# Changing the edges of an MLP stage in an encoder kernel: split rooms, PSUM banks, put-off sums and a free order

## The chip, the cores and the metric

The kernel runs on one core of a Trainium2 chip. The metric is the device time of one execution in microseconds. The kernel before took 2067.26 us, the median of three runs (2062.96 to 2069.44).

## The reference

It is a trunk of two layers over 256 tokens of width 2048. Each layer is a pre-norm token mixer (12 heads, in layer 0 neighbourhood attention and in layer 1 grouped-query attention) beside 4 cross-attention heads into 256 memory tokens, one output projection, and then the part that this change is about, a squared-ReLU MLP of width 8192:

```python
for i in range(DEPTH):
    n = rms_norm(h, attn_norm[i])
    ...
    h = h + jnp.concatenate([mix, cross], axis=-1) @ w_o[i]
    n = rms_norm(h, mlp_norm[i])
    h = h + jnp.square(jax.nn.relu(n @ w_up[i])) @ w_down[i]
return rms_norm(h, final_norm)
```

All inputs and weights are float32.

## The kernel before

**Number format.** Every matrix product is done as three matmuls in fp32r. Each operand is split into a high part (a copy rounded to fp32r, on ACT, line 370) and a low part (the difference, on DVE, line 371), and hi x hi, hi x lo and lo x hi are summed in PSUM. A `split` is that pair. The weights come from DRAM as float32 in chunks of 1 MB, each in two halves of 128x1024, and every weight half is split before the PE can use it.

**The up projection.** `up_grains` makes 128 rows of the MLP's inner layer: `load` fetches a 1 MB chunk `raw_U` through the SP queue into one of two tiles, `prep(hf)` splits a half of it into `uh` and `ul`, and `run(hf)` does 24 matmuls of 128x256 with the normalized activations hT into the sum `ps_u`. `half_of_side` gives the rooms for the halves: `uh` and `ul` have two rooms each. `squared` then takes the sum (Relu on line 811, square on line 812, both on ACT) and from each second chunk makes sums and differences of the blocks (line 821, DVE) and splits them into `a`. `PARTS` is 8: an MLP is eight parts of eight such chunks (`PK`).

**The down projection.** For seven of the eight parts it is done by Strassen's scheme: four blocks of weights `b` and their combinations give seven products `p1` to `p7`, each with a PSUM bank of its own. `down_grains` does one step: `load` fetches `b` (two tiles), `pre` makes three sums in `t` (lines 845, 847, 848, on DVE) and adds one block to another with an accumulating DMA on the POOL queue (line 846), `prep_first` splits `b` into `bh` and `bl`, `prep_second` splits `t` into `th` and `tl` (one room each), and two runs do the products of FIRST (p3, p1, p2, p5: twelve matmuls of 128x512) and of SECOND (p7, p6, p4: nine). When a half of the columns ends, `taken` empties the banks: three products go straight into the residual h (line 905), four into the shared sums `z` (line 916). At the last time for a half, `folded` combines the z tiles into h with eight operations on DVE (lines 927 to 934). The eighth part goes through `plain_grains`, ordinary products of 128x512 into the sums `ps_m`.

**The order of the work.** `plan` is a list of grains. `run_all` walks it and calls each grain's load, pre and prep a fixed number of grains ahead (`SOON`: 8, 5 and 4), then its `run` and `after`. `later(n, fn)` puts a function off by n grains. First come the 16 halves of part 0 (the "first part" in this text), then 56 fused steps, each of a `down_grains` pair for one part and an `up_grains` pair for the next, in this order:

```python
            plan.extend((down[0], up[0], up[1], down[1]))
```

The framework then plans the order of the instructions on each engine by its own estimates of their times. `pin` (`keep_in_program_order`) holds instructions in the order in which they were written, `past(fn, split)` holds what `fn` issues behind a given split on its engine. In the fused steps the first matmul of each product and each k tile is pinned; in the first part nothing is. Each engine runs its own list strictly in the order so planned.

**PSUM.** Eight banks. Outside the MLP's fused steps, the pool `ps_acc` (four banks, opened first) holds sums such as `ps_u` of part 0 and `ps_m`, and `ps_att` (four banks) holds what attention and the transposes need. For the fused steps both are closed and `ps_sums` takes their place, with one bank for each of p4, p3, p1, p2, p5, p7, p6 in this order and one for `up`. A tile in a new pool waits for the last use of the tile whose bank it takes. A pool of SBUF works in the same way: `mlp` takes the space of `ring` and `cat` when they are closed.

Of the kernel before, what the change touches and what calls it, by code (L numbers as in the profile page):

```python
# [17 lines left out]
P = 128  # L18
D = 2048
SEQ = 256  # L20
# [21 lines left out]
MOVING_AT = 160  # L42

LAST_AT = 224

STILL_AT = 64

# [58 lines left out]
def encoder_kernel(ctx: ExitStack, tc: tile.TileContext, t: dict, out: bass.AP):  # L106
# [20 lines left out]
    class at:  # L127
        pass

    def open_sums():  # L130
        at.acc = opened("ps_acc", space=bass.MemoryType.PSUM, bufs=4)
        at.att = opened("ps_att", space=bass.MemoryType.PSUM, bufs=4)

    def open_ring():
        at.ring = opened("ring")
# [232 lines left out]
    def split(dst_hi, dst_lo, src):  # L368

        first = nc.scalar.activation(dst_hi, src, AF.Copy)  # L370
        return first, nc.vector.tensor_tensor(dst_lo, src, dst_hi.bitcast(F32), op=ALU.subtract)  # L371
# [393 lines left out]
    def half_of_side(raw, hf, place=0):  # L765
        s = slice(place // 4, place // 4 + HALF)
        tiles = tuple(at.side.tile([P, HALF + 64], F32R, tag=n, bufs=2, name=n)[:, s] for n in ("uh", "ul"))
        box.setdefault("splits", []).append(split(*tiles, raw[:, hf * HALF : (hf + 1) * HALF]))
        return tiles
# [3 lines left out]
        nc.sync.dma_start(raw, src)  # L773
        return raw

    def up_grains(layer, part, m):
        own = {}

        def load():
            own["raw"] = loaded(t[f"w_up{layer}"][part * PK + m], "U")  # L780

        def prep(hf):
            own[hf] = half_of_side(own["raw"], hf)

        def run(hf):
            if hf == 0:
                if part == 0:
                    own["ps"] = at.acc.tile([P, 512], F32, tag="acc", name="ps_u")[:, :SEQ]
                else:
                    own["ps"] = at.sums.tile([P, 512], F32, tag="up", name="ps_u")[:, :SEQ]  # L790
            products(own["ps"], box["hT"], hf * (KT // 2), KT // 2, *own.pop(hf), keep_order=part > 0)

        def after():
            if part == 0 and m == 0:
                closed("cat", "ring")
                at.mlp = opened("mlp")
                box["z"] = [at.mlp.tile([P, 4, 512], F32, tag=f"z{q}", name=f"z{q}") for q in range(2)]
                box["z_set"] = set()
# [26 lines left out]
        if part == PARTS - 1 and m == PK - 1 and layer == 1:  # L825
            later(2, load_gf)

    def down_grains(layer, part, n, begins, ends):

        q, j = part % 2 ^ n // STEPS, n % STEPS  # L830
        own = {}

        def load():
            own["b"] = at.side.tile([P, 4, 512], F32, tag="b", bufs=2, name="b")
            nc.sync.dma_start(own["b"].rearrange("p a b -> p (a b)"),
                              t[f"w_pair{layer}"][(part * 2 + q) * STEPS + j])

        def behind(fn):

            return (lambda: past(fn, box["splits"][-4])) if part == 0 and n < 2 else fn  # L840

        def pre():

            b, s = own["b"], at.side.tile([P, 3, 512], F32, tag="T", bufs=2, name="t")
            nc.vector.tensor_tensor(s[:, 0, :], b[:, 3, :], b[:, 0, :], op=ALU.add)  # L845
            nc.gpsimd.dma_start(b[:, 3, :], b[:, 1, :], accum_op=ALU.add)  # L846
            nc.vector.tensor_tensor(s[:, 1, :], s[:, 0, :], b[:, 1, :], op=ALU.add)
            nc.vector.tensor_tensor(s[:, 2, :], s[:, 1, :], b[:, 2, :], op=ALU.add)
            own["t"] = s

        def prep_first():
            own["first"] = tuple(at.mlp.tile([P, CH], F32R, tag=x, name=x) for x in ("bh", "bl"))
            split(*own["first"], own["b"].rearrange("p a b -> p (a b)"))

        def prep_second():
            own["second"] = tuple(at.mlp.tile([P, 3 * 512], F32R, tag=x, name=x) for x in ("th", "tl"))
            split(*own["second"], own["t"].rearrange("p a b -> p (a b)"))

        def run(which, products):
            if part == n == 0 and which == "first":  # L860
                closed("ps_att", "ps_acc")
                at.sums = opened("ps_sums", space=bass.MemoryType.PSUM)
                box["ps"] = {}
                box["unused"] = set()
            hi, lo = own.pop(which)
            a = box["a", part, j]
            for name, ai, bi in products:
                if begins:
                    sum_of(name)
                ps, s = box["ps"][name], slice(bi * 512, (bi + 1) * 512)  # L870
                pin(nc.tensor.matmul(ps, a[:, 0, ai, :], hi[:, s], start=begins, stop=False))  # L871
                nc.tensor.matmul(ps, a[:, 0, ai, :], lo[:, s], start=False, stop=False)  # L872
                nc.tensor.matmul(ps, a[:, 1, ai, :], hi[:, s], start=False, stop=ends)  # L873

        def after(products):
            if ends:
                for name, _, _ in products:
                    taken(q, name)

        def after_second():  # L880
            after(SECOND)
            if ends:
                box["z_set"].add(q)
            if ends and (part, n) in FOLDS:
                folded(q)

        return [Grain(lambda: run("first", FIRST), lambda: after(FIRST), load, behind(pre), behind(prep_first), SOON),
                Grain(lambda: run("second", SECOND), after_second, None, None, behind(prep_second), SOON)]

    def sum_of(name):  # L890

        if not box["ps"]:
            for x in ("p4", "p3", "p1", "p2", "p5", "p7", "p6"):
                box["ps"][x] = at.sums.tile([P, 512], F32, tag=x, name=x)
                box["unused"].add(x)
        if name in box["unused"]:
            box["unused"].remove(name)
        else:
            box["ps"][name] = at.sums.tile([P, 512], F32, tag=name, name=name)

    def columns_of(i, q, b):
        return h[:, i, q * 1024 + b * 512 : q * 1024 + (b + 1) * 512]

    def add_scaled(hs, src, factor):
        nc.vector.scalar_tensor_tensor(hs, src, factor, hs, op0=ALU.mult, op1=ALU.add)
# [14 lines left out]
    DIRECT = {"p2": (1, 0), "p3": (1, 1), "p4": (0, 0)}  # L920
    SHARED = ("p1", "p5", "p6", "p7")

    def folded(q):

        z1, z5, z6, z7 = (box["z"][q][:, n, :] for n in range(4))
        inv, ninv = box["inv"], box["ninv"]
        add_scaled(columns_of(1, q, 0), z1, inv[:, 1:2])
        nc.vector.tensor_tensor(z6, z6, z1, op=ALU.subtract)
        nc.vector.tensor_tensor(z7, z6, z7, op=ALU.subtract)
        nc.vector.tensor_tensor(z6, z6, z5, op=ALU.add)  # L930
        add_scaled(columns_of(1, q, 1), z6, inv[:, 1:2])
        add_scaled(columns_of(0, q, 0), z7, inv[:, 0:1])
        nc.vector.tensor_tensor(z7, z7, z5, op=ALU.add)
        add_scaled(columns_of(0, q, 1), z7, ninv[:, 0:1])

    def plain_grains(layer, nb):

# [17 lines left out]
        def begin():  # L955
            if nb == 0:
                closed("ps_sums")
                open_sums()
            w.ps = [at.acc.tile([P, 512], F32, tag="acc", name="ps_m") for _ in range(NT)]

        def run(n):
# [24 lines left out]
    SOON = (8, 5, 4)  # L986
    STEPS_OF = [(p, n) for p in range(PARTS - 1) for n in range(2 * STEPS)]
    HALF_OF = [p % 2 ^ n // STEPS for p, n in STEPS_OF]
    FOLDS = {STEPS_OF[max(i for i, x in enumerate(HALF_OF) if x == q)] for q in range(2)}

    def add_mlp(layer):
        for m in range(PK):
            plan.extend(up_grains(layer, 0, m))
        for x, (p, n) in enumerate(STEPS_OF):
            begins = x == 0 or HALF_OF[x - 1] != HALF_OF[x]
            ends = x == len(STEPS_OF) - 1 or HALF_OF[x + 1] != HALF_OF[x]
            up, down = up_grains(layer, p + 1, n), down_grains(layer, p, n, begins, ends)
            plan.extend((down[0], up[0], up[1], down[1]))
        for nb in range(4):
            plan.extend(plain_grains(layer, nb))  # L1000

# [301 lines left out]
```

## Time and profile before

| | |
|---|---|
| median of 3 runs | 2067.26 us (2062.96 to 2069.44) |
| profiled execution | 2065.99 us, of it 2064.2 us from the first to the last instruction |
| mean granted TensorE clock | 0.995 |
| PE (matmul) busy | 2034.1 us, 99% |
| DVE busy | 1663.7 us, 81% |
| ACT busy | 1243.8 us, 60% |
| moved by DMA | 433.83 MB, 210 GB/s in the mean |

The page slices the span and gives busy time for each engine. A matmul's busy time includes its way through the array, so that consecutive matmuls overlap and an almost unbroken busy time does not say that the PE is at its peak; the spacing of the starts does. In layer 0 the first part runs from about 438 us to 492, the fused steps to 1067 and the plain part after that; in layer 1 the same stages are at about 1374 to 1428, to 2008, and on to the end.

### The profile page before, as it was taken

Reading aid. Unit: us, or ns where it says so; the run is one execution under the profiler, and the core shown is the slowest. Engines: PE = TensorE matmul, PEld = TensorE weight load, DVE = VectorE, ACT = ScalarE, POOL = GpSimd, SP = SyncE. Lnnn points to the kernel's source line nnn. Section 1 sums busy time; section 2 is a strip of 40 time slices with the busy share of each in tenths; the row PEclk is TensorE's granted clock in tenths of the full one; section 3 lists DMA queues with packets and bytes.
Section 4 is the critical chain, followed back from the end, with each engine's and each line's share of the span. In section 5 each row is a group of like instructions: output and inputs, shape, how many; then the busy total and the mean of one; then the engine's idle time right before and its main releaser. Section 6 shows DMA issues by size and latency. Waiting matters only on the chain.

```text
span 2064.2 us, 32575 instructions
## 1 busy us (share of the span) xinstructions
PE 2034.1 (99%) x13116; PEld 1844.1 (89%) x13116; DVE 1663.7 (81%) x2030; ACT 1243.8 (60%) x1616; POOL 119.3 (6%) x144
## 2 busy tenths in 40 slices
PE   9999999999999999999999999999999999999988
PEld 8999999888999999999988888888999999999976
DVE  6767666557999999999996668657999999999985
ACT  6654444455666666666655557555666666666654
POOL 0000000000000000001000001000000000000000
PEclk9999999999999999999999999999999999999999
DMA  7855555726777777777765544626777777777762
GB/s 281 306 182 175 184 182 168 291 76 210 230 228 237 222 245 229 222 239 228 230 196 203 178 177 143 228 95 204 228 232 230 231 230 233 225 235 229 229 212 103
DMA packets 77303, 433.83 MB, mean 210 GB/s; under 512 B 8672, under 2 KB 10336, under 8 KB 29664
## 3 DMA queue, kind: packets, MB, share of 16 engines
q1 hardware_dynamic: 59760, 399.25, 55.5%
q0 software_dynamic: 16816, 31.46, 8.7%
q8 instruction: 102, 1.67, 0.3%
q10 hardware_dynamic: 576, 1.05, 0.1%
q14 instruction: 49, 0.40, 0.1%
HBM read 398.17 MB, written 4.19 MB: 195 GB/s over the span
## 4 chain that ended last, share of the span: by engine, by line
PE 73%; DVE 1%; DMA 1%; issue 1%; ACT 1%; POOLq 0%; POOL 0%; ACTq 0%; DVEq 0%
PE ps_u L286 31%; PE p L871 9%; PE p L872 9%; PE p L873 8%; PE ps_m L265 5%; PE ps_m L268 5%; PE ps_m L269 5%; DMA b<-b 1%; DVE ul L371 1%; PE pt_n L388 0%; PE pt_a L447 0%; DMA raw_U<-in_w_up 0%; ACT bh L370 0%; ACT uh L370 0%; PE pt_h L1087 0%
## 5 line engine op out<-in xcount | busy, mean ns | idle before, releaser
L286 PE MATMUL ps_u<-hT,uh 128*128 128x256 f32 x4096 | 713.3, 278 | 0.8 <-ACT uh L370 0.6
L286 PEld LDWEIGHTS ps_u<-hT,uh 128*128 128x128 f32 x4096 | 629.2, 189 | 10.7 <-ACT uh L370 1.6
L286 PE MATMUL ps_u<-hT,ul 128*128 128x256 f32 x2048 | 569.5, 278 | 8.1 <-DVE ul L371 8.1
L370 ACT ACTIVATE uh<-raw_U 128x1024 fp32r<-128x1024 f32 x278 | 294.6, 1061 | 309.6 <-PE ps_u L286 276.3
L286 PEld LDWEIGHTS ps_u<-hT,ul 128*128 128x128 f32 x2048 | 386.8, 189 | 9.8 <-DVE ul L371 9.6
L371 DVE TENSOR_TENSOR ul<-raw_U,uh 128x1024 fp32r<-128x1024 f32 x278 | 338.9, 1221 | 60.9 <-ACT uh L370 60.7
L371 DVE TENSOR_TENSOR lo<-raw,hi 128x1024 fp32r<-128x1024 f32 (+1 forms) x215 | 255.6, 1194 | 144.2 <-ACT hi L370 143.0
L370 ACT ACTIVATE hi<-raw 128x1024 fp32r<-128x1024 f32 (+1 forms) x215 | 222.1, 1039 | 201.0 <-PE ps_m L269 111.8
L370 ACT ACTIVATE bh<-b 128x2048 fp32r<-128x2048 f32 x112 | 215.2, 1922 | 122.3 <-PE p L873 87.7
L371 DVE TENSOR_TENSOR bl<-b,bh 128x2048 fp32r<-128x2048 f32 x112 | 256.3, 2289 | 22.2 <-ACT bh L370 22.1
L371 DVE TENSOR_TENSOR tl<-t,th 128x1536 fp32r<-128x1536 f32 x112 | 196.7, 1756 | 42.1 <-ACT th L370 41.1
L370 ACT ACTIVATE th<-t 128x1536 fp32r<-128x1536 f32 x112 | 166.7, 1488 | 38.7 <-PE p L873 38.7
L871 PE MATMUL p<-bh,a_s 128*128 128x512 f32 x448 | 175.2, 391 | 3.5 <-ACT c L811 1.9
L872 PE MATMUL p<-bl,a_s 128*128 128x512 f32 x448 | 175.0, 391 | 1.8 <-DVE bl L371 1.8
L873 PE MATMUL p<-bh,a_s 128*128 128x512 f32 x448 | 175.3, 391 | 0.0
L846 POOL DMA_DIRECT2D b<-b x112 | 97.0, 866 | 1157.0 <-DVE t L845 902.7
L286 PE MATMUL ps_s<-nT,hi 128*128 128x256 f32 x896 | 158.1, 279 | 0.0
L286 PEld LDWEIGHTS ps_s<-nT,hi 128*128 128x128 f32 x896 | 136.3, 188 | 0.2
L871 PE MATMUL p<-th,a_s 128*128 128x512 f32 x336 | 131.4, 391 | 0.0
L872 PE MATMUL p<-tl,a_s 128*128 128x512 f32 x336 | 131.2, 390 | 0.0
L873 PE MATMUL p<-th,a_s 128*128 128x512 f32 x336 | 130.7, 389 | 0.0
L286 PE MATMUL ps_s<-nT,lo 128*128 128x256 f32 x448 | 124.9, 279 | 0.0
(233 smaller groups left out, 3361.9 us busy)
## 6 DMA issues: line engine op xcount, KB each, us to landing
raw_U<-in_w_up SPq DMA_DIRECT2D x128, 1024.0 KB, 5.1
b<-in_w_pair SPq DMA_DIRECT2D x112, 1024.0 KB, 5.1
raw<-in_w_o SPq DMA_DIRECT2D x32, 1024.0 KB, 5.0
b<-b POOLq DMA_DIRECT2D x112, 256.0 KB, 3.4
raw<-in_w_b SPq DMA_DIRECT2D x21, 1024.0 KB, 5.1
raw<-in_w_av SPq DMA_DIRECT2D x12, 1024.0 KB, 5.0
raw<-in_w_aq SPq DMA_DIRECT2D x12, 1024.0 KB, 4.9
raw<-in_w_ak SPq DMA_DIRECT2D x12, 1024.0 KB, 4.9
```

The source lines that it names most:

```text
L265: first = nc.tensor.matmul(w.ps[i], ah, hi[:, s], start=st, stop=False)
L268: nc.tensor.matmul(w.ps[i], ah, lo[:, s], start=False, stop=False)
L269: nc.tensor.matmul(w.ps[i], al, hi[:, s], start=False, stop=sp)
L286: ins = nc.tensor.matmul(ps, x[:, s], acts[:, k, part], start=k == n == 0, stop=k == KT - 1 and n == 2)
L370: first = nc.scalar.activation(dst_hi, src, AF.Copy)
L371: return first, nc.vector.tensor_tensor(dst_lo, src, dst_hi.bitcast(F32), op=ALU.subtract)
L846: nc.gpsimd.dma_start(b[:, 3, :], b[:, 1, :], accum_op=ALU.add)
L871: pin(nc.tensor.matmul(ps, a[:, 0, ai, :], hi[:, s], start=begins, stop=False))
L872: nc.tensor.matmul(ps, a[:, 0, ai, :], lo[:, s], start=False, stop=False)
L873: nc.tensor.matmul(ps, a[:, 1, ai, :], hi[:, s], start=False, stop=ends)
```

## The change

- Part 0's halves, counted 0 to 15, use a third room where the count modulo 3 is 2. For half 2 it is a `b` tile (two tiles are shared with the down weights); for halves 5, 8, 11 and 14 it is the tiles `th` and `tl`, at an offset of 96 bytes (`U_AT`). The pool `mlp`, which holds `th` and `tl`, is opened before part 0's first matmuls instead of after its first chunk.
- In `ps_sums` the banks go by group: FIRST's four, and `up` with SECOND's three. In layer 0 the second group takes the four lower banks, in layer 1 the upper ones. When the pools of four are opened again after layer 0's MLP, `ps_att` is opened ahead of `ps_acc`, so the two change sides.
- `folded` issues its eight operations one at a time, one or two grains apart, each held behind a recent split.
- In the last four fused steps of each layer (from `LAST_HALF` on) no matmul is pinned, and the order of the grains is up, down, up, down.

```diff
+U_AT = 96
...
-    def open_sums():
-        at.acc = opened("ps_acc", space=bass.MemoryType.PSUM, bufs=4)
-        at.att = opened("ps_att", space=bass.MemoryType.PSUM, bufs=4)
+    def open_sums(layer=1):
+        for x in ("acc", "att")[:: 1 if layer else -1]:
+            setattr(at, x, opened(f"ps_{x}", space=bass.MemoryType.PSUM, bufs=4))
...
-    def up_grains(layer, part, m):
+    def up_grains(layer, part, m, fixed=False):
...
         def prep(hf):
-            own[hf] = half_of_side(own["raw"], hf)
+            if part == 0 and (2 * m + hf) % 3 == 2:
+                if m == 1:
+                    room = at.side.tile([P, 2, HALF], F32R, tag="b", bufs=2, name="u_b")
+                    own[hf] = room[:, 0], room[:, 1]
+                else:
+                    s = slice(U_AT // 4, U_AT // 4 + HALF)
+                    own[hf] = tuple(at.mlp.tile([P, 3 * 512], F32R, tag=x, name=f"u_{x}")[:, s] for x in ("th", "tl"))
+                box["splits"].append(split(*own[hf], own["raw"][:, hf * HALF : (hf + 1) * HALF]))
+            else:
+                own[hf] = half_of_side(own["raw"], hf)
         def run(hf):
+            if part == m == hf == 0:
+                closed("cat", "ring")
+                at.mlp = opened("mlp")
+                ...
             if hf == 0:
                 if part == 0:
                     own["ps"] = at.acc.tile([P, 512], F32, tag="acc", name="ps_u")[:, :SEQ]
                 else:
-                    own["ps"] = at.sums.tile([P, 512], F32, tag="up", name="ps_u")[:, :SEQ]
-            products(own["ps"], box["hT"], hf * (KT // 2), KT // 2, *own.pop(hf), keep_order=part > 0)
+                    own["ps"] = sum_of("up")[:, :SEQ]
+            products(own["ps"], box["hT"], hf * (KT // 2), KT // 2, *own.pop(hf), keep_order=fixed)
...
-    def down_grains(layer, part, n, begins, ends):
+    def down_grains(layer, part, n, begins, ends, fixed):
...
             if part == n == 0 and which == "first":
-                closed("ps_att", "ps_acc")
-                at.sums = opened("ps_sums", space=bass.MemoryType.PSUM)
-                box["ps"] = {}
-                box["unused"] = set()
+                open_strassen(layer)
...
-                pin(nc.tensor.matmul(ps, a[:, 0, ai, :], hi[:, s], start=begins, stop=False))
+                ins = nc.tensor.matmul(ps, a[:, 0, ai, :], hi[:, s], start=begins, stop=False)
+                if fixed:
+                    pin(ins)
...
             if ends and (part, n) in FOLDS:
-                folded(q)
+                folded(q, 1 if (part, n) == STEPS_OF[-1] else 2)
...
+    def open_strassen(layer):
+        closed(*[x for x in reversed(list(pools)) if x in ("ps_acc", "ps_att")])
+        at.sums = opened("ps_sums", space=bass.MemoryType.PSUM)
+        first = [x[0] for x in FIRST]
+        second = ["up"] + [x[0] for x in SECOND]
+        box["ps"], box["unused"] = {}, set()
+        for x in first + second if layer else second + first:
+            box["ps"][x] = at.sums.tile([P, 512], F32, tag=x, name="ps_u" if x == "up" else x)
+            box["unused"].add(x)
...
-    def folded(q):
+    def folded(q, gap):
...
+        for n, fn in enumerate((out(1, 0, z1, inv), add(z6, z6, z1, ALU.subtract), add(z7, z6, z7, ALU.subtract),
+                                add(z6, z6, z5), out(1, 1, z6, inv), out(0, 0, z7, inv), add(z7, z7, z5),
+                                out(0, 1, z7, ninv))):
+            later(1 + gap * n, lambda fn=fn: past(fn, box["splits"][-2]))
...
                 closed("ps_sums")
-                open_sums()
+                open_sums(layer)
...
+    LAST_HALF = max(i for i, x in enumerate(HALF_OF) if x != HALF_OF[-1]) + 1
...
-            up, down = up_grains(layer, p + 1, n), down_grains(layer, p, n, begins, ends)
-            plan.extend((down[0], up[0], up[1], down[1]))
+            fixed = x < LAST_HALF
+            up, down = up_grains(layer, p + 1, n, fixed), down_grains(layer, p, n, begins, ends, fixed)
+            plan.extend((down[0], up[0], up[1], down[1]) if fixed else (up[0], down[0], up[1], down[1]))
```

More of the change, by code (lines that the diff above doesn't have):

```diff
@@ L782, in prep @@
         def prep(hf):
-            own[hf] = half_of_side(own["raw"], hf)
-        def run(hf):
+            if part == 0 and (2 * m + hf) % 3 == 2:
[8 more added lines that the diff above has]
+                own[hf] = half_of_side(own["raw"], hf)
+        def run(hf):
+            if part == m == hf == 0:
+                closed("cat", "ring")
+                at.mlp = opened("mlp")
+                box["z"] = [at.mlp.tile([P, 4, 512], F32, tag=f"z{q}", name=f"z{q}") for q in range(2)]
+                box["z_set"] = set()
             if hf == 0:
@@ L789, in run @@
                 else:
-                    own["ps"] = at.sums.tile([P, 512], F32, tag="up", name="ps_u")[:, :SEQ]
-            products(own["ps"], box["hT"], hf * (KT // 2), KT // 2, *own.pop(hf), keep_order=part > 0)
+                    own["ps"] = sum_of("up")[:, :SEQ]
+            products(own["ps"], box["hT"], hf * (KT // 2), KT // 2, *own.pop(hf), keep_order=fixed)
         def after():
[L794 to L798, printed above, removed]
             squared(layer, part, m, own["ps"])
@@ L884, in after_second @@
             if ends and (part, n) in FOLDS:
-                folded(q)
+                folded(q, 1 if (part, n) == STEPS_OF[-1] else 2)
         return [Grain(lambda: run("first", FIRST), lambda: after(FIRST), load, behind(pre), behind(prep_first), SOON),
                 Grain(lambda: run("second", SECOND), after_second, None, None, behind(prep_second), SOON)]
+    def open_strassen(layer):
[7 more added lines that the diff above has]
+            box["unused"].add(x)
     def sum_of(name):
[L892 to L895, printed above, removed]
         if name in box["unused"]:
@@ L898, in sum_of @@
         else:
-            box["ps"][name] = at.sums.tile([P, 512], F32, tag=name, name=name)
+            box["ps"][name] = at.sums.tile([P, 512], F32, tag=name, name="ps_u" if name == "up" else name)
+        return box["ps"][name]
     def columns_of(i, q, b):
@@ L921, in encoder_kernel, with add, out @@
     SHARED = ("p1", "p5", "p6", "p7")
-    def folded(q):
+    def folded(q, gap):
         z1, z5, z6, z7 = (box["z"][q][:, n, :] for n in range(4))
         inv, ninv = box["inv"], box["ninv"]
[L927 to L934, printed above, removed]
+        def add(d, x, y, op=ALU.add):
+            return lambda: nc.vector.tensor_tensor(d, x, y, op=op)
+        def out(i, b, z, factor):
+            return lambda: add_scaled(columns_of(i, q, b), z, factor[:, i : i + 1])
+        for n, fn in enumerate((out(1, 0, z1, inv), add(z6, z6, z1, ALU.subtract), add(z7, z6, z7, ALU.subtract),
+                                add(z6, z6, z5), out(1, 1, z6, inv), out(0, 0, z7, inv), add(z7, z7, z5),
+                                out(0, 1, z7, ninv))):
+            later(1 + gap * n, lambda fn=fn: past(fn, box["splits"][-2]))
     def plain_grains(layer, nb):
```

## The prediction

> **What bounds the kernel now.** I read the page first, then the busy time of the engines by stage, then the PE's order of time wherever a stage had PE time missing, then the ACT, DVE and SP orders around those places.
>
> ```profile
> span 2064.2 us, 32575 instructions
> PE 2034.1 (99%) x13116; PEld 1844.1 (89%) x13116; DVE 1663.7 (81%) x2030; ACT 1243.8 (60%) x1616; POOL 119.3 (6%) x144
> ```
>
> The PE is the bound, so only its holes can be won. By stage (columns: length, then busy us and instructions of PE, PEld, DVE, ACT, POOL; granted clock, DMA share, GB/s):
>
> ```profile
> 495.37:1066.80 571.43, 571.43 (x3852) 525.40 (x3851) 528.28 (x561) 370.84 (x371) 46.14 (x53) 1.00 0.74 229
> 451.31:476.78 25.47, 25.47 (x219) 25.47 (x217) 17.04 (x24) 14.67 (x21) 1.05 (x1) 1.00 0.60 203
> 447.44:491.72 44.28, 39.39 (x312) 38.57 (x313) 32.77 (x46) 24.63 (x34) 2.80 (x3) 0.96 0.64 203
> 1383.34:1428.08 44.74, 39.55 (x312) 38.31 (x312) 2.90 (x8) 0.96 0.61 200
> ```
>
> (The last row counts the up matmuls alone.) Layer 0's fused up and down steps (571 us) have no hole, and the DVE is 92% busy there: 571.43 - 528.28 = 43 us of slack over about 56 steps, 0.8 us a step. The holes lie at the edges. In the first part 451.31 to 476.78 is nine undisturbed halves, 2.83 us each. The next two rows hold thirteen halves each, 36.8 us at that pace, but take 44.28 and 44.74: **7.5 us lost in layer 0, 7.9 in layer 1**. Where, on the PE (start, duration, then in brackets the idle time and what ended it):
>
> ```profile
> 482.48 0.38 PE L286 MATMUL ps_u<-hT,ul 128*128 128x256 f32 x1 [2.02 <-DVE ul L371]
> 493.18 0.50 PE L871 MATMUL p<-bh,a_s 128*128 128x512 f32 x1 [0.60 <-ACT c L811]
> 1428.08 0.50 PE L871 MATMUL p<-bh,a_s 128*128 128x512 f32 x1 [1.30 <-ACT c L811]
> 1066.57 0.39 PE L872 MATMUL p<-tl,a_s 128*128 128x512 f32 x1
> 1066.80 0.39 PE L873 MATMUL p<-th,a_s 128*128 128x512 f32 x1
> 1069.10 0.47 PE L265 MATMUL ps_m<-uh,a_p 128*128 128x512 f32 x1 [1.91 <-DVE h L905]
> 1981.66 0.39 PE L873 MATMUL p<-th,a_s 128*128 128x512 f32 x1
> 1983.61 0.50 PE L871 MATMUL p<-bh,a_s 128*128 128x512 f32 x1 [1.56 <-ACT bh L370]
> 1989.92 0.39 PE L873 MATMUL p<-bh,a_s 128*128 128x512 f32 x1
> 2007.70 0.39 PE L873 MATMUL p<-th,a_s 128*128 128x512 f32 x1
> 2010.00 0.71 PE L265 MATMUL ps_m<-uh,a_p 128*128 128x512 f32 x1 [1.91 <-DVE h L905]
> ```
>
> A 512-wide matmul starts 0.23 us after the one before (1066.57, 1066.80). So the start of the plain down stage loses 2.30 - 0.23 = **2.07 us in each layer**: its first sum sits in the bank that the last product of the step (p4) used, and waits for the DVE to empty it. Near the end of layer 1, 1981.66 to 1989.92 is twelve matmuls, 2.7 us at full pace, in 8.26: **5.5 us lost** to a late bh and what follows. The first product after the first part waits **0.6 us** in layer 0 for the Relu of the last up sum (493.18); in layer 1 that wait of 1.30 is already in the 7.9.
>
> After some of these holes the clock falls:
>
> ```profile
> 485.00:495.00 10.00, 7.48 (x38) 6.49 (x38) 8.20 (x13) 2.87 (x5) 0.87 (x1) 0.83 0.68 178
> 1064.00:1074.00 10.00, 8.09 (x41) 6.58 (x41) 8.98 (x13) 4.38 (x6) 0.00 (x0) 1.00 0.49 148
> 1416.00:1426.00 10.00, 7.16 (x44) 6.72 (x44) 10.00 (x11) 5.31 (x7) 1.63 (x2) 0.83 0.64 187
> 1981.00:1991.00 10.00, 6.62 (x25) 4.89 (x24) 7.41 (x8) 7.15 (x8) 0.00 (x0) 0.83 0.43 128
> 2006.00:2016.00 10.00, 8.09 (x29) 6.21 (x28) 8.32 (x12) 4.35 (x6) 0.00 (x0) 0.83 0.81 298
> ```
>
> A granted 0.83 over 10 us is 1.7 us lost. Three of the four dips lie inside losses already counted; the one at 2006 adds **1.7 us**. The same 2.07 us hole at 1066.80 cost no dip. All told: 7.5 + 0.6 + 7.9 + 2.07 + 2.07 + 1.7 + 5.5 = **27.3 us** that this change aims at.
>
> **The change part by part.**
>
> *Three rooms for the first part's halves.* No instruction is added; five of sixteen splits a layer write elsewhere (half 2 into a b tile; halves 5, 8, 11 and 14 into th/tl). The gain is lead. ACT and DVE orders (ACT's 440.95, 446.34 and 451.39 are splits):
>
> ```profile
> 440.95 1.06 ACT L370 ACTIVATE uh<-raw_U 128x1024 fp32r<-128x1024 f32 x1 [5.73 <-PE ps_u L286]
> 445.71 0.63 ACT L660 ACTIVATE sq<-h 128x512 bf16<-128x512 f32 x1 [1.15 <-DVE h L718]
> 446.34 1.04 ACT L370 ACTIVATE uh<-raw_U 128x1024 fp32r<-128x1024 f32 x1
> 451.39 1.06 ACT L370 ACTIVATE uh<-raw_U 128x1024 fp32r<-128x1024 f32 x1 [1.73 <-PE ps_u L286]
> 452.49 1.23 DVE L371 TENSOR_TENSOR ul<-raw_U,uh 128x1024 fp32r<-128x1024 f32 x1 [1.74 <-ACT uh L370]
> 477.05 1.92 ACT L370 ACTIVATE bh<-b 128x2048 fp32r<-128x2048 f32 x1 [1.25 <-DMA b<-b]
> 478.87 1.04 ACT L370 ACTIVATE uh<-raw_U 128x1024 fp32r<-128x1024 f32 x1
> 479.00 2.29 DVE L371 TENSOR_TENSOR bl<-b,bh 128x2048 fp32r<-128x2048 f32 x1 [1.93 <-ACT bh L370]
> 481.21 1.22 DVE L371 TENSOR_TENSOR ul<-raw_U,uh 128x1024 fp32r<-128x1024 f32 x1
> ```
>
> With two rooms a split starts when the PE leaves its room (451.39) and is ready 2.33 us later (452.49 + 1.23), against a half of 2.83: 0.5 us to spare. Two things overrun that. The squares of the attention sum stand before a split (445.71), and at the end bh and bl of the first down step do: bh waits 1.25 us for its accumulating DMA with uh behind it in ACT's order, and ul waits for bl; ul ends at 482.43 and the PE restarts at 482.48. A third room gives 2.83 us more, 3.3 in all. The bh wait plus bh is 3.2 us, bl 2.29, so one such overrun is just covered. The splits of halves 2 and 14 no longer need a room that the PE has just left. I take 1.5 us a layer as remaining (bounds: 0, and 4 if the bh order still bites once).
>
> What it costs elsewhere: the b tile of half 2 is held until the PE has done that half, so the load of the second b (before: with the attention stage) moves into the first part, to the SP queue between these:
>
> ```profile
> 448.67 28.02 SPq L773 DMA_DIRECT2D raw_U<-in_w_up  x6
> raw_U<-in_w_up SPq DMA_DIRECT2D x128, 1024.0 KB, 5.1
> ```
>
> Six loads were spread over 28 us at 5.1 each, and the first (448.67) waited for the fourth split. That one now takes half 0's room, free at 440.95, and ends 2.33 us later at 443.3, 5.4 us sooner; that hides one more 5.1 us load. If that cover is gone (the new load stands in front, waiting for its tile), one up load is late by up to 5.1 us less the 3.3 of lead, 1.8 us a layer. th of the first down step now waits until the PE has done half 14; it is used two down products and two up halves later, over 8 us, so nothing. The address offset U_AT and the new rooms change no matmul count; I take zero, bounded by the pace of halves in the fused steps (5.48 for two, below), 0.1 us a half either way, 2.6 us on 26.
>
> *PSUM banks by group, pools on alternating sides.* The first products (p3, p1, p2, p5) take the attention banks, idle since the last transposes; the second products and the up sum take the up banks. So 0.6 + 1.3 go; the next on those banks are the second products, two halves later. At the end the plain stage's sums take p3's and p1's banks, emptied while an up half (2.7) and the second products (nine matmuls, 2.05) still run; three direct DVE reads of about 0.7 fit in. So 2.07 twice and the dip of 1.7 go. Late next is the split of the plain weights, ready before (nothing waited on it). Taken whole.
>
> *Shared sums put off.* The eight DVE operations of a fold keep their number and size:
>
> ```profile
> 1967.29 0.69 DVE L928 TENSOR_TENSOR z<-z 128x512 f32<-128x512 f32 x1
> b<-b POOLq DMA_DIRECT2D x112, 256.0 KB, 3.4
> 1973.12 8.37 DMA b<-b
> 1973.68 0.33 SPq L773 DMA_DIRECT2D raw_U<-in_w_up  x1
> ```
>
> Spread over fifteen grains, they load a step with about 1.4 us instead of 5.6 in two. That matters for the late bh: its DMA was issued at 1973.12, 0.56 us before a 1 MB load, and took 8.37 us against a median of 3.4. Less DVE queue brings it forward by one or two operations, and down moves behind an up half (2.7 us more). 5.5 us if nothing of it returns; I take 4.5, since an issue so close to a load may recur.
>
> *Free order, up first, in the last four steps.* An up half moves in front of the first products. Moved with it are its load (ahead of b's on SP) and its split (ahead of bh and bl on ACT and DVE); the accumulating DMA on POOL is passed by nothing. At the switch b's load comes one load later (5.1 us) and its products one up half later, which its two tiles cover; after that the order is periodic again. The up sum has one bank, and its reuse comes 2.05 us (second products) instead of 4.8 after its last matmul. The PE's two up halves in the fused steps, and ACT:
>
> ```profile
> 1059.66 5.48 PE ps_u L286 x48
> 1959.42 1.06 ACT L370 ACTIVATE uh<-raw_U 128x1024 fp32r<-128x1024 f32 x1 [1.66 <-PE ps_u L286]
> 1960.38 0.36 ACT L811 ACTIVATE c<-ps_u 128x256 f32<-128x256 f32 x1
> ```
>
> The Relu ends 1.3 us after that uh, which starts when the last up matmul is done: 0.7 us to spare. I charge 0.25 us a step, 2 us in both layers (bounds: 0, and 3.9 us a step, below).
>
> Sum: 27.3 - 3.0 (first parts) - 1.0 (late bh) - 2.0 (free order) = 21.3; the profiled execution took 2065.99 (span 2064.2 and 1.8 around it), so 2044.7. The median, 2067.26, is 1.3 above that execution: **2046 us**.
>
> **A rule against this sum.** The dips above come only behind holes, of 1.9 to 2.3 us. The Trainium skill, "TensorE: Matmul & The Clock Gate", section "HAM oscillation — how this bites in real kernels", puts the limit at idle gaps over about 3.4 us. By that rule these holes would not be what lowers the clock, and closing them would not bring the dips back. The four rows at 0.83 speak for the holes, so this case's trace does not agree with the limit.
>
> **Rivals.**
>
> *The dips stay* (another cause): four times 1.7 = 6.8 us less, 2053. Against it: the fused steps, with no hole, stand at 1.00 for 571 us. Chance 0.04.
>
> *The first part keeps half its losses*, because bh, bl and the accumulating DMA still stand before the last splits, now earlier too, or the second b's load stands ahead of up loads: 7.7 us instead of 3.0, and the late bh returns with 4.5: 2055. For it: ACT and DVE are in order, and the 3.3 us of lead is about what bh takes. Chance 0.17.
>
> *The changes cancel*: free order loses 2 us a step (8 steps, 16 us): 2060 to 2066. Chance 0.07.
>
> *Slower.* Place: the start of each of the eight free steps. If ACT puts th or bh (1.9 us) before the Relu, the single up bank is not free, and each step has a hole like 482.48's (about 2.2 us lost) and its dip (1.7): 3.9 us x 8 = 31 against 23.3 won without free order: 2067.3 + 7.9 = 2075. It decides from about 3.7 us a step (23.3 + 6.2, over 8). Against it: ACT idled 1.66 us before 1959.42. Chance 0.06.
>
> *The forecast*, 2038 to 2050: 0.60. *Better than the sum's gain*, all 27 and more: 0.06.
>
> About 0.3%, 6.2 us, is what a measurement can tell from no change. Faster by more: 0.04 + 0.17 + 0.60 + 0.06 = 0.87; within: 0.07; slower: 0.06. The range 2037 to 2057 leaves out the ends of the cancelling and slower cases and most of the better one; the forecast's own is 2038 to 2050.
>
> **What would show it.** Right: the thirteen-half windows take 37 to 39 us; no wait on ul over 1 us in the first parts; ps_m begins 0.3 us after the last p at both ends; no 0.83 in any 10 us there. Wrong: waits of PE ps_u on ACT c or ul in the last four steps, a PE wait on raw_U, or matmuls from the th/tl or b rooms starting further apart than 0.118 us.

## The result and the profile after

The changed kernel takes **2040.55 us** (median of 4 runs, 2040.02 to 2042.54) against 2065.52 for the kernel before beside it: a ratio of 0.9879, 95% interval 0.986 to 0.9898. Measured again with other kernels, it took 2042.33 (2038.72 to 2043.74, ratio 0.9885, 0.987 to 0.99). The profiled execution of after took 2040.02 us, 26.0 less than that of before, and so did its span.

From the page of after (span, busy time, and the share of the chain that ended last by engine):

```profile
span 2038.2 us, 32567 instructions
PE 2023.9 (99%) x13116; PEld 1838.1 (90%) x13116; DVE 1661.1 (81%) x2030; ACT 1245.0 (61%) x1616; POOL 119.3 (6%) x144
PE 98%; DMA 1%; issue 0%; ACT 0%; DVE 0%; SPq 0%; POOLq 0%; POOL 0%; ACTq 0%; DVEq 0%
```

The same matmuls and nearly the same work on DVE and ACT; what went is time in which the PE stood or ran at half clock (in the profile of before the granted clock fell behind four holes, about 1.7 us each). The chain of after holds the PE for 98% of the span. The page of before has 73% there, but its chain, which is followed back from the end, breaks off at 471.97 us; of the part that it covers, the PE has 95%. What the PE still waited for (all of it: us in total, times, longest):

```profile
PE ps_s L289 <- ACT hi L373: 1.2, 2, 1.0
PE idle L176 <- POOL mhalf L170: 1.0, 1, 1.0
PE av L458 <- ACT pT L373: 1.0, 1, 1.0
PE ps_u L289 <- ACT c L824: 1.0, 1, 1.0
PE p L881 <- ACT bh L373: 0.8, 1, 0.8
PE ps_u L289 <- DVE ul L374: 0.6, 2, 0.3
```

The first three lie outside the MLP. The waits for room (ul, 8.1 us before) are two of 0.3; the waits of ps_m on h (3.8 us) are gone. The windows that answer to those shown of before:

```profile
446.90:484.02 37.12, 36.84 (x314) 36.62 (x313) 26.65 (x40) 23.45 (x33) 1.93 (x2) 1.00 0.71 228
1371.97:1409.18 37.21, 36.93 (x315) 36.52 (x313) 26.41 (x40) 23.45 (x33) 1.84 (x2) 1.00 0.68 224
485.00:495.00 10.00, 10.00 (x70) 9.20 (x69) 9.96 (x13) 6.82 (x10) 0.87 (x1) 1.00 0.72 206
1055.00:1065.00 10.00, 10.00 (x52) 8.51 (x51) 9.35 (x13) 5.44 (x7) 0.00 (x0) 1.00 0.45 152
1410.00:1420.00 10.00, 10.00 (x70) 9.21 (x69) 9.88 (x12) 6.83 (x10) 0.86 (x1) 1.00 0.84 228
1985.00:1995.00 10.00, 10.00 (x46) 8.29 (x45) 9.96 (x14) 5.13 (x7) 0.00 (x0) 1.00 0.86 305
```

The same thirteen halves take 37.12 and 37.21 us where they took 44.28 and 44.74, and in this profile no 10 us at the edges stands at 0.83. On the PE, the first product after the first part, and both starts of the plain stage:

```profile
483.91 0.28 PE L289 MATMUL ps_u<-hT,ul 128*128 128x256 f32 x1
484.02 0.39 PE L881 MATMUL p<-bh,a_s 128*128 128x512 f32 x1
1058.09 0.39 PE L885 MATMUL p<-th,a_s 128*128 128x512 f32 x1
1058.32 0.39 PE L268 MATMUL ps_m<-uh,a_p 128*128 128x512 f32 x1
1985.53 0.39 PE L885 MATMUL p<-th,a_s 128*128 128x512 f32 x1
1985.76 0.39 PE L268 MATMUL ps_m<-uh,a_p 128*128 128x512 f32 x1
```

Each follows at full pace (0.11 and 0.23 us). To see where the 26.0 us come from I divided each span at starts of PE rows: the first ps_u, the 22nd p, the first p of the fourth-last step, the last p and the first ps_m of each layer. Us:

```
stage                                  before    after    after, again
before layer 0's MLP                   437.86   437.78   438.02
first part and first fused step, L0     65.23    56.53    56.49
fused steps up to the last four, L0    522.92   522.92   522.92
last four steps, L0                     40.79    40.87    40.87
last p to first ps_m, L0                 2.30     0.23     0.23
plain part and attention between       304.66   304.53   304.54
first part and first fused step, L1     64.70    56.59    56.58
fused steps up to the last four, L1    522.92   522.92   522.92
last four steps, L1                     46.32    43.17    46.70
last p to first ps_m, L1                 2.30     0.23     0.23
from there to the end                   54.21    52.48    52.49
span                                  2064.21  2038.24  2041.97
```

So 8.70 + 8.11 from the first parts, 2.07 twice at the ends, 1.73 behind the second end, 3.15 in layer 1's last four steps: 25.8 of 26.0. The last of these is the only one that doesn't repeat.

### The profile page after: what moved, and what is told of

The parts are those of the page before. It is cut to its first block, busy times and chain, and to the rows that moved or that the text cites. A ratio compares the mean times of both kernels' runs of the same rounds, so it can differ in the third digit from the quotient of the medians.

```text
span 2038.2 us, 32567 instructions
## 1 busy us (share of the span) xinstructions
PE 2023.9 (99%) x13116; PEld 1838.1 (90%) x13116; DVE 1661.1 (81%) x2030; ACT 1245.0 (61%) x1616; POOL 119.3 (6%) x144
## 4 chain that ended last, share of the span: by engine, by line
PE 98%; DMA 1%; issue 0%; ACT 0%; DVE 0%; SPq 0%; POOLq 0%; POOL 0%; ACTq 0%; DVEq 0%
PE ps_u L289 34%; PE ps_s L289 10%; PE p L884 9%; PE p L885 9%; PE p L881 9%; PE ps_m L268 8%; PE ps_m L271 8%; PE ps_m L272 8%; PE pt_a L450 1%; PE pt_n L391 1%; DMA b<-b 0%; PE sc_ps L425 0%; PE av L458 0%; PE sc_ps L424 0%; PE sc_ps L426 0%
## 5 line engine op out<-in xcount | busy, mean ns | idle before, releaser
L289 PE MATMUL ps_u<-hT,uh 128*128 128x256 f32 x3936 | 682.4, 277 | 1.0 <-ACT c L824 1.0
L289 PEld LDWEIGHTS ps_u<-hT,uh 128*128 128x128 f32 x3936 | 602.3, 188 | 10.6 <-ACT c L824 1.4
L289 PE MATMUL ps_u<-hT,ul 128*128 128x256 f32 x1968 | 544.8, 277 | 0.6 <-DVE ul L374 0.6
L373 ACT ACTIVATE uh<-raw_U 128x1024 fp32r<-128x1024 f32 x268 | 284.1, 1061 | 269.5 <-PE ps_u L289 242.8
L289 PEld LDWEIGHTS ps_u<-hT,ul 128*128 128x128 f32 x1968 | 370.3, 188 | 1.2 <-DVE ul L374 1.0
L374 DVE TENSOR_TENSOR ul<-raw_U,uh 128x1024 fp32r<-128x1024 f32 x268 | 325.8, 1219 | 36.2 <-ACT uh L373 36.1
L885 PE MATMUL p<-bh,a_s 128*128 128x512 f32 x448 | 174.6, 390 | 0.0
L881 PE MATMUL p<-bh,a_s 128*128 128x512 f32 x448 | 170.9, 389 | 0.8 <-ACT bh L373 0.8
```

Of the source, the lines that this page charges most:

```text
L289: ins = nc.tensor.matmul(ps, x[:, s], acts[:, k, part], start=k == n == 0, stop=k == KT - 1 and n == 2)
L881: ins = nc.tensor.matmul(ps, a[:, 0, ai, :], hi[:, s], start=begins, stop=False)
```

## The experiments

First each part undone by itself, on the kernel after; then the late transfer; then parts alone, on the kernel before.

**Two rooms again.**

```diff
-            if part == 0 and (2 * m + hf) % 3 == 2:
+            if False:
```

> The changed kernel with the third room taken away (all halves of the first part in the two uh/ul rooms), the rest kept. Theory (the two-room limit is what made the PE wait in the first parts; the banks only removed the waits on the Relu, 0.6 and 1.3 us): each first part is longer by 8.4 less its bank share, 7 to 8 us, so about 15 us slower than the changed kernel, 2055 to 2056, and waits of PE ps_u on DVE ul of about 2 us come back. Rival (the banks and the unpinned PE order carry the gain, the rooms are incidental): within 4 us of the changed kernel, about 2041 to 2044.

2054.76 us (2051.91 to 2056.83; ratio to before 0.9954, 0.9938 to 0.997). The first parts take 64.05 and 64.12. PE waits, and one of its rows:

```profile
PE ps_u L289 <- DVE ul L374: 9.6, 6, 2.0
483.50 0.39 PE L289 MATMUL ps_u<-hT,ul 128*128 128x256 f32 x1 [2.01 <-DVE ul L374]
```

The third room is worth 7.5 us in each layer, by ending the waits on ul and the fall of the clock behind the last of them (one of about 1.7 us in each layer). What else differs in this profile, 1.19 us more ahead of layer 0's MLP and 0.60 less in layer 1's last four steps, differs as much between kernels that have the room.

**The old banks.**

```diff
-        for x in ("acc", "att")[:: 1 if layer else -1]:
+        for x in ("acc", "att"):
...
-        for x in first + second if layer else second + first:
+        for x in ("p4", "p3", "p1", "p2", "p5", "p7", "p6", "up"):
```

> The changed kernel with the banks as before (pools always in the order acc, att; order p4, p3, p1, p2, p5, p7, p6, up). Theory: the 2.07 us wait at the start of each plain stage comes back (4.1), and the waits on the Relu at the end of each first part (0.6 and 1.3), 6 us in all, with up to 1.7 us for each fall of the clock behind a hole: 2046 to 2049. Rival (with the free order the second products no longer end last, so the old banks would not hurt): 2041 to 2043. On the clock: if holes of about 2 us lower it only by where they fall, one, both or none of the two ends show a granted 0.83; if a gap must exceed 3.4 us, none does.

2051.18 us (2049.11 to 2052.89; 0.9934, 0.9918 to 0.9951). PE waits, then two windows of 10 us:

```profile
PE ps_m L268 <- DVE h L924: 4.4, 2, 2.2
PE p L881 <- ACT c L824: 1.9, 2, 1.3
1059.00:1069.00 10.00, 7.81 (x28) 6.04 (x27) 7.21 (x10) 2.77 (x5) 0.00 (x0) 0.83 0.63 211
1994.00:2004.00 10.00, 7.81 (x28) 6.07 (x27) 7.26 (x10) 3.08 (x5) 0.00 (x0) 0.83 0.83 303
```

Both ends are 2.58 us again instead of 0.23, the waits for Relu are back (0.91 and 1.49 us of the first parts), and now the clock falls behind both ends (plain part and attention 306.24, the last stage 54.09): 4.7 + 2.4 + 3.3 = 10.4 us. The remaining 2.4 of the span's 12.9 is layer 1's last four steps, 45.53, of which below. The theory's 2046 to 2049 was short, and this profile is the slowest of its four runs.

**The shared sums at once.**

```diff
-            later(1 + gap * n, lambda fn=fn: past(fn, box["splits"][-2]))
+            fn()
```

> The changed kernel with the eight operations of a fold issued at once, as before. Theory (the late bh of the third last step in layer 1 comes from an accumulating DMA that is triggered just ahead of a 1 MB load; the DVE queue only shifts it by 1 to 2 us): the last four steps of layer 1 take 43 to 46 us (43.2 with the change, 46.3 before), layer 0's stay at 41: 0 to 3 us slower, 2040 to 2043. Rival (the DVE queue is what makes bh late): over 3 us slower and a new hole in layer 0 too.

2043.88 us (2040.18 to 2045.26; 0.9899, 0.9883 to 0.9916), span 2038.4, every stage within 0.3 us of after's (layer 1's last four steps 43.13). Putting the sums off shows in one place only: layer 0's last four steps take 41.08 without it and 40.87 with it. But the median is 1.6 to 3.3 us above the two of after, and the profile is the fastest of its four runs; whether the sums or the late transfer below make that difference is not settled.

**The fixed order to the end,** run twice.

```diff
-            fixed = x < LAST_HALF
+            fixed = True
```

> The changed kernel with all fused steps pinned and in the order down, up, up, down. Theory (the free order gives the late bh another 2.7 us, and costs nothing elsewhere): layer 1's last four steps go from 43.2 to 45 to 47 us, with a granted 0.83 behind the hole: 2 to 4 us slower, 2042 to 2045. Rival (the put-off fold did it, the free order is idle or costs its 0.25 us a step): same or up to 2 us faster, 2038 to 2041.

> The changed kernel with the fixed order in the last half, a second time, because the late transfer took 9.1 us in its first profile and between 7.0 and 9.2 us in the others. Theory (at the same landing time the free order saves 2 us or so, and what a profile shows beyond that is the landing's own scatter and the half clock behind a hole of over 2 us): 2043.5 us, layer 1's last four steps 45 to 48 us by how long the transfer takes. Rival (the free order saves nothing, the two kernels differ by the scatter alone): 2041 us.

2043.68 us (2042.66 to 2044.62), and 2042.42 (2041.24 to 2043.39), against 2040.55 and 2042.33 of after, which was measured in other sets of runs. Layer 0's last four steps take 40.79 both times, as before; layer 1's 47.79 and 44.88. From the 4.6 us of the first pair of profiles I first read that the free order saves 4.6 us there. The next experiments show that most of that was scatter.

**The late transfer.** The third of layer 1's last four steps, the last but one (the expectations call it the third-last), waits for bh, which waits for b, which waits for POOL's adding transfer. The chain of after (start, duration, what) and 10 us at the hole; then the same transfer and the same 10 us in after's second profile:

```profile
1952.29 0.61 DVE t L858
1952.90 0.03 POOLq L859
1952.93 1.15 issue
1954.08 0.01 POOLq L859
1954.09 7.64 DMA b<-b
```

```profile
1962.00:1972.00 10.00, 8.25 (x53) 6.88 (x52) 8.17 (x9) 9.32 (x9) 0.00 (x0) 1.00 0.43 136
```

```profile
1954.29 9.15 DMA b<-b
1962.00:1972.00 10.00, 7.61 (x22) 5.38 (x21) 6.45 (x7) 6.52 (x8) 0.00 (x0) 0.67 0.34 110
```

POOL starts the transfer 1.20 us after the add t has ended in every profile that has it (here 1.15 of it is "issue", time in which the engine waits for nothing that the profile shows); for the twin, the same step of layer 0, it is 0.53. So it goes out 0.56 us ahead of a 1 MB load, here on SP:

```profile
1954.65 0.33 SPq L776 DMA_DIRECT2D raw_U<-in_w_up  x1
```

and lands after 6.9 to 9.2 us, differently from run to run, against a median of 3.4; the twin, 1.23 us ahead of its load, took 3.9 to 4.2 us. The third room brought two more such neighbours, in all ten profiles that have it: in the first part of layer 1 a transfer 0.23 us ahead of a load (after: 1405.72) took 7.2 to 7.9 us, in that of layer 0 one 0.93 us ahead took 4.4 to 5.2. So the long landing is not peculiar to the one step; it also came where another load followed within 0.6 us, though the places may differ in more than that. The PE waits for neither of the two new ones. At 7.64 the PE stands 0.95 and 1.13 us; at 9.15 it stands 2.47 us in one piece and the clock falls to 0.67 over 10 us. Three kernels beside a second run of after:

> The changed kernel itself, as a yardstick for the two beside it: 2040.6 us, with the wait of layer 1's third-last chunk on its pair weights still there (0.8 us on bh, 1.0 us on c) and 43.2 us for layer 1's last four steps.

*x_pool8*, eight more fills on POOL at the start, to move the late start to another place:

```diff
+    for _ in range(8):
+        nc.gpsimd.memset(mhalf, -0.5)
```

> Eight further one-line fills by the POOL engine at the start, after which everything POOL does stands eight instructions later in its program. Theory (the late start of the adding transfer of layer 1's third-last step hangs on the place in POOL's program): the transfers that start 0.9 to 1.8 us late after their add are other ones, that transfer starts 0.53 us after its add, 1.2 us ahead of the 1 MB load and not 0.56, lands in about 4 us and not 7.6; the wait on bh goes, layer 1's last four steps take 40.9 us and not 43.2, and the time is 2038.5 us. Rival (POOL waits there for something of the kernel's own): the same transfer starts 1.2 us late again, 43.2 us, 2040.6 us.

*x_dve_add*, the sum of that one step by VectorE; *x_dve_fixed*, the same with the fixed order to the end:

```diff
-            nc.gpsimd.dma_start(b[:, 3, :], b[:, 1, :], accum_op=ALU.add)
+            if layer == 1 and part == PARTS - 2 and n == 2 * STEPS - 2:
+                nc.vector.tensor_tensor(b[:, 3, :], b[:, 3, :], b[:, 1, :], op=ALU.add)
+            else:
+                nc.gpsimd.dma_start(b[:, 3, :], b[:, 1, :], accum_op=ALU.add)
```

> In layer 1's third-last step alone the sum that POOL's adding transfer makes is made by one VectorE add. Theory (that transfer's landing, and nothing else, makes the wait on bh and the wait on c behind it): both go, layer 1's last four steps take 40.9 us, the span is 2036 us and the time 2038.5 us. Rival (the two waits come from VectorE's queue, which splits late there anyway): the add of 0.5 to 1 us comes on top, the waits stay or grow, 43.2 to 44.2 us and 2040.6 to 2041.6 us.

> The changed kernel with the old, fixed order in the last half too, and with the one sum of layer 1's third-last step made by VectorE, so that no transfer is late there. Theory (the free order pays only by filling the wait for that transfer): layer 1's last four steps take 40.8 us as in layer 0, and the time is that of the free order with the same VectorE sum, 2038.5 us. Rival (the free order is faster of itself, the last half's products standing better in it): 0.5 to 2 us more in each layer, 2040 to 2042 us.

x_pool8: 2040.56 us (2039.69 to 2043.17), and my theory of the place fell, for a shift by eight at least. The start still comes 1.21 us after the add, and the landing takes 7.8 us:

```profile
1954.99 0.86 POOL L861 DMA_DIRECT2D b<-b  x1 [14.82 <-DVE z L950]
1955.55 0.33 SPq L778 DMA_DIRECT2D raw_U<-in_w_up  x1
```

The name in the bracket, an add on z that runs on DVE right behind t, does not explain it: in layer 0 the same add stands in the same place and the start is on time. Why POOL starts late there stays open.

x_dve_add: **2038.56 us** (2037.31 to 2039.19), against 2042.33 of after and 2040.56 of x_pool8, which keeps the transfer, beside it; layer 1's last four steps 40.91. x_dve_fixed: **2037.74** (2037.62 to 2038.16; 0.987, 0.9855 to 0.9885); 40.79. Windows at the place, first the fixed order, then the free one:

```profile
1962.00:1972.00 10.00, 10.00 (x70) 9.21 (x69) 9.44 (x10) 6.38 (x8) 0.86 (x1) 1.00 0.75 237
```

```profile
1962.00:1972.00 10.00, 10.00 (x70) 9.18 (x69) 9.26 (x10) 6.51 (x7) 0.86 (x1) 1.00 0.74 237
```

So the transfer alone makes the hole; one add in its place takes it away, with no new PE wait in the MLP:

```profile
1955.38 0.68 DVE L860 TENSOR_TENSOR b<-b 128x512 f32<-128x512 f32 x1
```

Without the transfer the free order saves nothing: 40.79 against 40.91. What it saves with the transfer there, by the landing time of each profile:

```
us to landing    6.9-7.1        7.5-7.6        8.4-8.5        9.1-9.2
fixed order      44.88          43.89          46.32, 46.40   47.79
free order       42.57, 43.13   43.63, 43.17   45.53          46.70
```

0.3 to 2.3 us at like landings (rows of all kernels run here, with 43.35 at 7.8 left over), and between the medians 0.1 and 3.1 us. The landing does not fix the time alone: 44.88 is longer than 43.89 though its transfer landed sooner, because the clock fell there (1966.70 in that profile, 1.7 us) and not in the other. So most of the 2.3 is clock. The free order fills part of a wait that should not be there.

**Parts alone, on the kernel before.** The edits are those parts of the diff of the change; the put-off sums alone were not run.

> The third room alone, on the kernel before. Theory (the parts add up): 7.5 us less in each layer's first part, 2050 us against 2065; waits for ul of 2.2 us gone, the ends still 2.30 us each, the waits for Relu still there. Rival (with the old banks the waits for Relu come in place of the waits for room and take back half): 2057 us.

> The new order of the PSUM banks alone, on the kernel before. Theory (the parts add up): each end 0.23 us and not 2.30, the half clock in the last stage gone (1.7 us), the two waits for Relu in the first parts gone (0.6 and 1.3 us): 5.9 to 7.8 us less, 2057 to 2059 us. Rival (what the first parts win on Relu they lose again to the room waits, and the late transfer eats the rest): 2061 us.

> The free order of the last half alone, on the kernel before. Theory (the free order lets other products fill the wait on the late pair weights): layer 1's last four steps fall from 46.3 to about 43.2 us, layer 0's stay at 40.8, nothing else moves: 2062.4 us against 2065.5. Rival (it pays only with the new banks): the 5.5 us hole stays, 2065.5 us.

Beside 2064.31 of before, the rooms alone give 2051.91 us (2050.19 to 2053.72; 0.9939, 0.9926 to 0.9951), the banks alone 2054.65 (2052.49 to 2057.13; 0.9953, 0.9941 to 0.9966). Their gains of 12.4 and 9.7 make 22.1 of the whole change's 22.4 to 25.0: they add up within the scatter of a few us. The rooms' waits, then the banks':

```profile
PE ps_m L266 <- DVE h L916: 3.8, 2, 1.9
PE p L882 <- ACT c L822: 1.9, 2, 1.3
PE ps_u L287 <- DVE ul L372: 0.6, 2, 0.3
```

```profile
PE ps_u L287 <- DVE ul L372: 9.4, 6, 2.0
```

Each part takes its own waits and leaves the other's. The rooms give 2.6 us less than the 15.0 expected: 7.84 and 6.55 in the first parts, and in this profile 1.6 us go back because the clock fell behind the first end as well. The banks gave more than either theory said. In the profile their two ends, the last stage and the first parts make 4.1 + 1.7 + 1.5; 2.4 more lie in layer 1's last four steps, where the transfer landed in 7.53 us and not 8.37; so far as its landing scatters, that is chance.

The free order alone: 2065.77 us against 2064.68 (1.0009, 1.0 to 1.0018). My theory (3 us less) fell for the time. The profile, the fastest of the eleven runs, doesn't show why: its span is 2.6 us shorter than that of before, as layer 1's last four steps fall from 46.32 to 43.63. What it shows against the free order is that the ends grow:

```profile
PE ps_m L265 <- DVE h L907: 5.0, 2, 2.5
```

2.91 us from the last p to the first ps_m instead of 2.30, twice: 1.2 us. Behind the first the clock falls, which it did not in the profile of before, and behind the second it no longer does, so the clock cancels. On the new banks that wait does not exist. What takes the rest of the gain in the timed runs stays open.

## Why the prediction was right, point by point

The forecast was 2046 us within 2037 to 2057, and faster; it came to 2040.55. The likeliest case (2038 to 2050) held, and its two main mechanisms, rooms and banks, are shown. The profiled execution was forecast at 2044.7 and took 2040.02, and 2043.74 in the second profile of after; the gain of 21.3 us was 26.0 and 22.2. In the first, 3.8 us more at the first parts and 2.0 of a charge for the free order that did not come stand against 1.35 less at the late bh; the second lost 3.5 us again to a later landing, so how near the sum came is in part luck. By its terms:

- *The first parts*: 13.0 us forecast (16.0 of holes less 1.5 a layer), 16.8 measured. The charge was the mistake: in each layer one hole of 0.45 us is left, in half 4 (0.28 of it waiting, below), where before had none, and not a repeat of the bh order. The forecast windows of 37 to 39 us came out at 37.12 and 37.21, so they gave 14.7 of the 15.4 us counted in them. The other 2.1 us lie outside: 0.45 in each layer in halves 1 and 2, ahead of the windows; 0.90 in layer 0's first twelve products, where the sum counted 0.6; 0.2 and 0.1 behind them. The 16.0 us counted as holes were thus 1.5 us short.

```profile
450.39 0.39 PE L289 MATMUL ps_u<-hT,ul 128*128 128x256 f32 x1 [0.28 <-DVE ul L374]
```

- *Loads*: the up load that I moved to 443.3 starts at 443.21, the second b load comes behind it at 445.85, and the PE waits for neither. Halves in the new rooms keep the pace of the others. Zero was right.

```profile
443.21 0.33 SPq L776 DMA_DIRECT2D raw_U<-in_w_up  x1
445.85 0.33 SPq L848 DMA_DIRECT2D b<-in_w_pair  x1
```

- *The banks*: 2.07 twice and a dip of 1.7 forecast, 2.07 twice and 1.73 measured. Undoing them brought each back, and a dip behind the other end too; that the profile of before had one dip at the ends and not two hung on where its holes fell (last section).
- *The late bh*: 4.5 of 5.5 us forecast; 3.15 in one profile, -0.4 in the other. Here the step failed in its mechanism: "Less DVE queue brings it forward". The transfer goes out at the same 0.56 us ahead of the load as before, with the sums put off or not. What the free order does fill is 0.3 to 2.3 us. My caution "an issue so close to a load may recur" was the right half of it.
- *The shared sums*: counted as what frees DVE for that bh; there no effect was seen.
- *The free order*: charged 2.0 us; in four steps it cost 0.1 us with the sums put off (40.87 against 40.79 in layer 0, 40.91 against 40.79 without the late transfer) and 0.3 without (41.08). The waits that would have shown the charge, on c or ul in the last four steps, are absent but for the one behind the late bh.
- *The step from the profiled time to the median*, 1.3 us up, was noise: 2067.26 was a median of three, and a later set of 15 runs of before has its at 2064.68.

Of the rivals, *the first part keeps half* fell with the windows, *slower* and *the changes cancel* with the last four steps. *The dips stay* fell too: behind the ends that have no hole there is no dip in any profile. The limit of about 3.4 us in the Trainium skill ("TensorE: Matmul & The Clock Gate", "HAM oscillation — how this bites in real kernels") does not fit these traces either: holes of 2.07 to 2.68 us at the ends were followed by a dip in six of the eight that the profiles of before, old banks, rooms alone and free order alone hold. Nor did the dips come "only behind holes, of 1.9 to 2.3 us", as the prediction has it: the one in 1981 to 1991 came behind two shorter waits, of 1.56 us (in its rows) and 1.82 us (on bl, at 1985.94).

## What to carry to other kernels

Count an in-order PE's holes by place, from the starts of its rows, and price a change by the holes it takes; on this kernel that sum held to 5 us of 26 with the two parts that mattered adding up. A hole behind a DMA has a price that scatters from run to run: look at the same wait in several profiles before crediting an edit with it, and ask first whether the transfer can go (one VectorE add of 0.68 us gained 2.0 to 3.8 us). Do the same with a fall of the clock: whether a hole of 2 us brings one differs between runs of one kernel. A reordering that helps by filling a wait is worth nothing once the wait is gone.

## What the runs showed of the hardware

- An adding transfer of 256 KB on POOL's queue takes 3.4 us in the median. With a 1 MB load issued behind it, it took 3.9 to 4.2 us when the load came 1.23 us later, 4.4 to 5.2 at 0.93, 6.9 to 9.2 at 0.56 (twelve profiles) and 7.2 to 7.9 at 0.23 (ten profiles).
- The price of a hole is not linear: 0.95 + 1.13 us left the clock at 1.00 over those 10 us, 2.47 us in one piece took it to 0.67.
- Which holes bring such a fall can be read from the profiles. Each fall of the clock (dip) behind a hole lasts 3.41 us, or twice that, at a granted 0.50, hence the 1.7 us. Within one profile the falls start whole multiples of 3.413 us apart: in that of before at 487.72, 1419.56, 1986.17 and 2010.06, which are 273, 166 and 7 such steps. So the falls lie on a grid of 3.413 us, and it lies differently in each profile. Here are the two equal holes of 2.07 us in that profile, divided on its grid (length, busy us of PE and the other engines, and third from the end the clock):

```profile
1064.57:1067.98 3.41, 2.62 (x14) 1.91 (x13) 2.43 (x4) 2.86 (x5) 0.00 (x0) 1.00 0.01 2
1067.98:1071.40 3.42, 2.30 (x10) 1.97 (x11) 3.42 (x6) 0.47 (x1) 0.00 (x0) 1.00 0.78 249
2006.65:2010.06 3.41, 1.50 (x8) 0.95 (x6) 3.29 (x5) 2.64 (x5) 0.00 (x0) 1.00 0.95 334
2010.06:2013.48 3.42, 3.42 (x8) 2.67 (x9) 3.39 (x6) 0.00 (x0) 0.00 (x0) 0.50 0.83 297
```

  The hole before 1069.10 falls into two stretches, in which the PE stands 0.8 and 1.1 us, and no dip follows. The one before 2010.00 falls into one, 1.9 us, and the next stretch is at half clock. Counted in this way in all fourteen profiles, from 20 us to the last stage, and outside of falls already begun, each of 19 stretches in which the PE stood 1.91 us or more was followed by a fall, and none of 58 with 0.4 to 1.60 us; between lie two, 1.78 with a fall and 1.90 without. In the first 20 us it is less sharp: 1.52 us brought one and 1.58 none. This was read off these profiles afterwards; no run was made to test it.
